# Experts' stage: router scores by token half, expert list before gates, residual and g2 moved into the PSUM sums

## The chip, the cores and the metric

The kernel runs on one core of one Trainium2 chip. The metric is the device time of one execution in microseconds (us), as the median of several executions; a profiled execution of its own gives the trace. Engine names in rows: PE is TensorE (PEld its weight loads), DVE is VectorE, ACT is ScalarE, POOL is GpSimd, SP is SyncE, whose queue (SPq) issues the weight loads.

## The reference, cut to what matters

The program runs two transformer blocks on 256 tokens of width 1024. The change touches only the last part, the mixture of experts of the second block and the final norm. `x` is the residual, `g2` one of six vectors of 1024 from the conditioning input, and everything is float32.

```python
h = rms_norm(x, norm2_w[l]) * (1.0 + sc2[:, None]) + sh2[:, None]
x = x + g2[:, None] * moe(h, w_router[l], router_bias[l], w_gate[l], w_up[l], w_down[l],
                          ws_gate[l], ws_up[l], ws_down[l])
return rms_norm(x, final_norm_w)
...
scores = jax.nn.sigmoid(xt.astype(jnp.float32) @ w_router.astype(jnp.float32))
sel = scores + router_bias.astype(jnp.float32)
group_score = lax.top_k(sel.reshape(M, N_GROUPS, N_EXPERTS // N_GROUPS), 2)[0].sum(-1)
_, gidx = lax.top_k(group_score, TOPK_GROUPS)
...
_, eidx = lax.top_k(jnp.where(emask, sel, -jnp.inf), TOP_K)
wts = jnp.take_along_axis(scores, eidx, axis=-1)
wts = wts / jnp.sum(wts, axis=-1, keepdims=True) * ROUTE_SCALE
...
routed = ...   # per token: sum over its 8 of 64 experts of gate * (silu(x w_gate) * (x w_up)) w_down
shared = (jax.nn.silu(xt @ ws_gate) * (xt @ ws_up)) @ ws_down
return (routed.reshape(M, D) + shared).reshape(B, T, D)
```

## The kernel before

Tokens lie in two halves of 128 (index `tt`). The function `moe` (line 1479 on) writes the instructions of PE, DVE, ACT and SP in program order: each of these engines runs its own list in the order in which the code issues it, and an instruction that waits holds up everything behind it on that engine.

The stage around the change runs in this order:

1. The normed tokens `h` are transposed into `hT` (`turn_in`), token half 0 first. The shared expert's first product (`shared_up(tt, b)`, line 1565; `b` counts four blocks of weights `wg`) starts for half 0 while half 1 is still normed.
2. The router scores (line 1617, PSUM tile `prt`) are one product of all 256 tokens with 64 experts. DVE copies them (`lg`, line 1623), PE turns them back to token rows (`prtT`), and ACT takes the sigmoid (`sc`, line 1628). Beside that ACT copies `h` into `hs[0]` and POOL computes the rest `hs[1]` (lines 1619 and 1620), which the gathers need later.
3. DVE picks groups and experts in some 30 small instructions: from `sel` (line 1651) to the mask `mk` (line 1684), then the gates (lines 1686 to 1691).
4. PE counts how many tokens each expert has (`ppos`, lines 1698 to 1702, from `mb`). DVE ranks the experts (`perm`), PE writes the list `plist` (lines 1774 and 1775), and DVE turns it into addresses `lst` (line 1779). SP reads `lst` (line 1825) before it can issue a load of an expert that is not one of the first three. A few small DVE instructions up to `moreu` (line 1788) say whether a rarely taken overflow branch is needed.
5. The shared expert is finished in between: `swiglu` (ACT at line 1576, DVE at line 1577), `turn` (two PE transposes `phT`, line 1583) and `shared_down`, which opens the four PSUM sums `psh` (named `py` in the rows).
6. `tables` and `gather` build the first unit's tokens (`pv`, line 1742; `pga`, line 1757), and `run` goes through the units: 25 units of up to 128 rows, of one to four experts each. A unit has four blocks of up products (`gu_unit`, line 1572), the down products two blocks (line 1591), and `combine` (line 1854), which adds it into the four PSUM sums. Its loads go through a ring of SBUF buffers in a fixed order: SP's next load waits until PE is done with the buffer it goes to.
7. At the end DVE and POOL multiply the four sums by `g2` (`mod[5]`) and add them to `x` (lines 1927 and 1929), and `final` norms `x` and writes it out.

Of the kernel before, what the change touches and what calls it, by code (L numbers as in the profile page):

```python
# [19 lines left out]
P = 128  # L20
# [1458 lines left out]
def moe(e, a, x, m, late, out):  # L1479
# [123 lines left out]
    for b in range(3):  # L1603
        shared_up(0, b)
# [9 lines left out]
    wr = wr.rearrange("p (c n) -> p c n", c=NC8)  # L1614
    p = ps.tile([P, 512], F32, tag="mm", name="prt", bufs=e.mm_bufs)
    for c in range(NC8):
        nc.tensor.matmul(p[:, :T], wr[:, c], hT[:, c], start=c == 0, stop=c == NC8 - 1)
    for tt in range(2):
        nc.scalar.activation(hs[0][:, tt], h[tt], AF.Copy)
        nc.gpsimd.tensor_sub(hs[1][:, tt], h[tt], hs[0][:, tt].bitcast(F32))  # L1620
    shared_up(0, 3)
# [8 lines left out]
    for b in range(4):  # L1630
        shared_up(1, b)
# [35 lines left out]
    hsh.append(turn(swiglu(pg[0])))  # L1667
    shared_down(0, 0)
# [16 lines left out]
    gate = pool.tile([P, 2, NE], F32, name="gate")  # L1685
    nc.vector.tensor_mul(gate, sc, mk)
    gsum = pool.tile([P, 2], F32, name="gsum")
    nc.vector.tensor_reduce(gsum, gate, axis=AX.X, op=OP.add)
    nc.vector.reciprocal(gsum, gsum)
    nc.vector.tensor_tensor(gate, gate, gsum[:, :, None].to_broadcast([P, 2, NE]), op=OP.mult)  # L1690
    nc.vector.tensor_scalar(gate, gate, 2.5, None, op0=OP.mult)

# [12 lines left out]
    shared_down(0, 1)  # L1705
# [70 lines left out]
    hsh.append(turn(swiglu(pg[1])))  # L1776
# [11 lines left out]
    nc.vector.tensor_copy(moreu, more)  # L1788
    for tt in range(2):
# [28 lines left out]
    def run(units, acc=(), new=None, ready=()):  # L1818
# [52 lines left out]
        for u in range(len(units) + 1):  # L1871
# [37 lines left out]
            if done is not None:  # L1909
# [12 lines left out]
        v = pool.tile([P, NC8, T], F32, tag="ehT", name=uid(e, "v"))  # L1922
        for tt in range(2):
            half = [slice(n * 512, (n + 1) * 512) for n in range(2)]
            vs = [v[:, 4 * tt + 2 * n:4 * tt + 2 * n + 2].rearrange("p a b -> p (a b)") for n in range(2)]
# [5 lines left out]
    def final():  # L1931
        for tt in range(2):
# [7 lines left out]
            for s in half:  # L1940
                nc.vector.scalar_tensor_tensor(o[:, s], x[tt][:, s], r, fw[:, s], op0=OP.mult, op1=OP.mult)
                nc.sync.dma_start(out[tt * P:(tt + 1) * P, s], o[:, s])

    run(units, psh, first_group, pre)
    final()
# [4 lines left out]
    if e.overflow:  # L1950
        with tc.If(nc.values_load(moreu[:, 5:6], min_val=0, max_val=T) > 0):
# [5 lines left out]
            with tc.If(v[2] > 0):  # L1957
                run([shared((r, 64), (r + 1, 64), base=64) for r in range(MID, LIGHT, 2)] 
# [6 lines left out]
            final()  # L1965
# [94 lines left out]
```

## Time and profile before

| what | value |
|---|---|
| median of 3 runs (lowest, highest) | 1731.15 us (1728.81, 1735.82) |
| the profiled execution's own time | 1730.54 us |
| its span in the trace | 1728.7 us |
| PE busy / PE weight loads busy | 1643.9 us (95%) / 1292.7 us (75%) |
| DVE busy / ACT busy / POOL busy | 1117.3 us (65%) / 745.1 us (43%) / 162.2 us (9%) |

The span is the profiled execution's time from its first to its last instruction; the own time is 1.8 us above it. The stage of the change, from the transposed tokens of half 0 to the first up product of an expert, takes from 1289.0 to 1325.8 us; the units run from there to about 1714 us, and the end takes the last 15 us.

### The profile page before, as it was taken

The numbers are of one execution on the slowest core, as the hardware profiler recorded it, in microseconds if no ns is written. First come the engines' busy times: TensorE is split into PE (matmuls) and PEld (weight loads), VectorE is DVE, ScalarE is ACT, GpSimd is POOL, SyncE is SP. The second block draws the span as 40 slices with busy tenths as digits, with TensorE's granted clock in tenths as the row PEclk, the third lists the DMA queues.
The fourth block names the chain that finished last, engine by engine and source line by source line (L and its number), as shares of the span: only waits on it lengthen the run. The fifth ranks groups of instructions, "written<-read, shape, count | busy, mean of one in ns | idle before, by whom it ended". The sixth has DMA issues, their size and how long they took to land.

```text
span 1728.7 us, 29531 instructions
## 1 busy us (share of the span) xinstructions
PE 1643.9 (95%) x11301; PEld 1292.7 (75%) x11301; DVE 1117.3 (65%) x2212; ACT 745.1 (43%) x1217; POOL 162.2 (9%) x84
## 2 busy tenths in 40 slices
PE   7999898999999999999899998998999999999996
PEld 7888798899989999787788876987875544444442
DVE  6765789994989999877777767689653111111113
ACT  4576444444544444444454455655542222222212
POOL 0000001232112122000000003024001000000000
PEclk9999999999999999999999999999999999999998
DMA  7442744456545555587888855442067799999994
GB/s 263 145 135 62 221 157 157 155 169 191 151 131 161 170 171 172 176 287 269 300 285 286 289 162 163 146 147 76 23 266 273 273 408 409 408 409 408 409 406 159
DMA packets 108118, 390.91 MB, mean 226 GB/s; under 512 B 12656, under 2 KB 12944, under 8 KB 107840
## 3 DMA queue, kind: packets, MB, share of 16 engines
q1 hardware_dynamic: 106128, 384.58, 63.7%
q0 software_dynamic: 976, 2.82, 0.6%
q8 instruction: 91, 1.49, 0.4%
q10 hardware_dynamic: 864, 1.53, 0.3%
q14 instruction: 59, 0.48, 0.1%
HBM read 386.79 MB, written 2.10 MB: 225 GB/s over the span
## 4 chain that ended last, share of the span: by engine, by line
PE 67%; DVE 17%; DMA 9%; issue 4%; ACT 3%; POOL 0%; DVEq 0%; SPq 0%; ACTq 0%
PE pgu L1572 10%; PE acc L696 8%; DMA raw<-in_w_ada 7%; PE py L1591 5%; PE pu L80 5%; PE pu L81 5%; PE pu L82 5%; DVE wlo L67 4%; PE pga L1757 3%; PE py L1854 3%; PE pg L642 2%; PE pmv L82 1%; PE pmv L80 1%; ACT whi L66 1%; PE pmv L81 1%
## 5 line engine op out<-in xcount | busy, mean ns | idle before, releaser
L66 ACT ACTIVATE whi<-raw 128x1024 fp32r<-128x1024 f32 x361 | 379.5, 1054 | 299.0 <-PE pu L81 138.5
L67 DVE TENSOR_TENSOR wlo<-raw,whi 128x1024 fp32r<-128x1024 f32 x315 | 385.2, 1226 | 81.3 <-ACT whi L66 80.3
L82 PE MATMUL pu<-pxT,wlo 128*128 128x256 f32 x1024 | 288.7, 282 | 11.6 <-DVE wlo L67 8.8
L80 PE MATMUL pu<-pxT,whi 128*128 128x256 f32 x1024 | 290.9, 284 | 0.7 <-ACT whi L66 0.7
L81 PE MATMUL pu<-pxT,whi 128*128 128x256 f32 x1024 | 287.5, 281 | 0.0
L696 PE MATMUL acc<-whi,hh 128*128 128x512 f32 x1008 | 279.6, 395 | 6.4 <-ACT hh L66 4.2
L696 PEld LDWEIGHTS acc<-whi,hh 128*128 128x128 f32 x1008 | 189.0, 189 | 51.3 <-DVE hh L67 5.2
L82 PEld LDWEIGHTS pu<-pxT,wlo 128*128 128x128 f32 x1024 | 194.0, 189 | 14.1 <-DVE wlo L67 10.9
L80 PEld LDWEIGHTS pu<-pxT,whi 128*128 128x128 f32 x1024 | 194.0, 189 | 0.9 <-ACT whi L66 0.9
L81 PEld LDWEIGHTS pu<-pxT,whi 128*128 128x128 f32 x1024 | 194.0, 189 | 0.0
L1572 PE MATMUL pgu<-raw,xg 128*32 128x512 f32 (+2 forms) x988 | 183.4, 597 | 0.0
L67 POOL TENSOR_TENSOR wlo<-raw,whi 128x1024 fp32r<-128x1024 f32 x46 | 128.1, 2788 | 499.6 <-ACT whi L66 498.1
L696 PE MATMUL acc<-wlo,hh 128*128 128x512 f32 x504 | 157.6, 393 | 2.2 <-DVE wlo L67 2.2
L66 ACT ACTIVATE hh<-H 128x256 fp32r<-128x256 f32 x126 | 52.6, 418 | 173.4 <-PE acc L696 171.6
L1572 PEld LDWEIGHTS pgu<-raw,xg 128*32 128x32 f32 (+2 forms) x988 | 52.4, 124 | 86.5 <-issue 74.9
L696 PEld LDWEIGHTS acc<-wlo,hh 128*128 128x128 f32 x504 | 94.8, 189 | 23.7 <-DVE wlo L67 3.8
L67 DVE TENSOR_TENSOR yl<-py,yh 128x512 fp32r<-128x512 f32 x50 | 34.6, 692 | 107.1 <-ACT yh L66 107.1
L1591 PE MATMUL py<-raw,th 128*32 128x512 f32 (+2 forms) x508 | 93.7, 596 | 0.5 <-ACT th L1585 0.5
L781 DVE SCALAR_TENSOR_TENSOR ada<-raw,cs,ada 128x1024 f32<-128x1024 f32 x48 | 61.5, 1282 | 41.0 <-DMA raw<-in_w_ada 40.9
L1577 DVE SCALAR_TENSOR_TENSOR hh<-hh,sv,pgu 128x256 f32<-128x256 f32 x25 | 12.0, 479 | 117.1 <-ACT hh L1576 117.1
L1760 ACT ACTIVATE xg<-pga 128x256 f32<-128x256 f32 (+1 forms) x104 | 39.1, 376 | 110.7 <-PE pga L1757 106.6
L1757 PEld LDWEIGHTS pga<-S,hs 128*128 128x128 f32 x416 | 54.8, 189 | 36.7 <-issue 36.0
(560 smaller groups left out, 2853.7 us busy)
## 6 DMA issues: line engine op xcount, KB each, us to landing
raw<-in_w_gu SPq DMA_DIRECT2D x187, 512.0 KB, 10.1
raw<-in_peer_u SPq DMA_DIRECT2D x128, 512.0 KB, 3.6
raw<-in_peer_v SPq DMA_DIRECT2D x128, 512.0 KB, 4.5
raw<-in_w_dn SPq DMA_DIRECT2D x91, 512.0 KB, 10.1
raw<-in_w_ada SPq DMA_DIRECT2D x48, 512.0 KB, 4.7
raw<-in_w_in_a SPq DMA_DIRECT2D x24, 512.0 KB, 3.9
raw<-in_w2a SPq DMA_DIRECT2D x17, 512.0 KB, 4.2
raw<-in_w_out SPq DMA_DIRECT2D x16, 512.0 KB, 3.5
```

The costliest lines, as they stand in the source:

```text
L66: e.nc.scalar.activation(hi, src, AF.Copy)
L67: (eng or e.nc.vector).tensor_sub(lo, src, hi.bitcast(F32))
L80: nc.tensor.matmul(out, lh, rh, start=first, stop=False)
L81: nc.tensor.matmul(out, lh, rl, start=False, stop=False)
L82: nc.tensor.matmul(out, ll, rh, start=False, stop=last)
L696: nc.tensor.matmul(acc[tt][n], h[l][:, s], w[r][:, n * 512:(n + 1) * 512], start=j == order[0] and i == 0, stop=j == order[-1] and i == 2)
L781: nc.vector.scalar_tensor_tensor(mod[n], w, cs[:, c:c + 1], mod[n], op0=OP.mult, op1=OP.add)
L1572: nc.tensor.matmul(pg[t], xx[:, c, t], ws[i][:, k * 512:(k + 1) * 512], start=c == 0, stop=c == NC8 - 1)
L1591: nc.tensor.matmul(py[q][t], th[:, k, t], w[i][:, q * 512:(q + 1) * 512], start=k == 0, stop=last and k == 1)
L1757: nc.tensor.matmul(p[:, :n].rearrange("p u n -> p (u n)"), hs[i][:, tt, q * P:(q + 1) * P], S[:, tt, :n].rearrange("p u n -> p (u n)"), st ...
L1760: nc.scalar.activation(xg[:, q, :n], p[:, :n], AF.Copy)
L1854: nc.tensor.matmul(acc[tt][n], St[:, tt * P:(tt + 1) * P], y[:, n * 512:(n + 1) * 512], start=first and v == 0 and w == 0, stop=v == len(u ...
```

## The change

The code changes in five places. The scores are computed by token half: half 0 ahead of the shared expert's first products, half 1 right after its transposes. The copies to `hs` go behind the sigmoid and an activation-table change. The shared products that stood ahead of the scores' way back are spread behind it. The gates, the shared down weights' multiplication by `g2` (new, in place, two 128x1024 instructions) and the first `swiglu` go behind the expert list. The residual `x` enters the PSUM sums by a product with the identity, each unit's result is multiplied by `g2` before it is split and added, and `final` reads the sums in PSUM.

```diff
-    for b in range(3):
+    def scores(tt):
+        for c in range(NC8):
+            nc.tensor.matmul(p[:, tts[tt]], wr[:, c], hT[:, c, tts[tt]], start=c == 0, stop=c == NC8 - 1)
+    scores(0)
+    for b in range(2):
         shared_up(0, b)
...
-    for c in range(NC8):
-        nc.tensor.matmul(p[:, :T], wr[:, c], hT[:, c], start=c == 0, stop=c == NC8 - 1)
-    for tt in range(2):
-        nc.scalar.activation(hs[0][:, tt], h[tt], AF.Copy)
-        nc.gpsimd.tensor_sub(hs[1][:, tt], h[tt], hs[0][:, tt].bitcast(F32))
-    shared_up(0, 3)
+    scores(1)
...
     warm(e, AF.Silu, sc[:, 0, 0:1])
-    for b in range(4):
-        shared_up(1, b)
+    for tt in range(2):
+        nc.scalar.activation(hs[0][:, tt], h[tt], AF.Copy)
+        nc.gpsimd.tensor_sub(hs[1][:, tt], h[tt], hs[0][:, tt].bitcast(F32))
+    for tt, b in ((0, 2), (0, 3), (1, 0)):
+        shared_up(tt, b)
...
     def shared_down(tt, k):
         if k == 0:
...
-        dn_block(psh[tt], hsh[tt], k, [(slice(0, P), 0)], [wd[k]], last=False)
+            for n in range(2):
+                nc.tensor.matmul(psh[tt][n], e.ident, x[tt][:, n * 512:(n + 1) * 512], start=True, stop=False)
+        for n in range(2):
+            nc.tensor.matmul(psh[tt][n], hsh[tt][:, k], wd[k][:, n * 512:(n + 1) * 512], start=False, stop=False)
...
-    hsh.append(turn(swiglu(pg[0])))
-    shared_down(0, 0)
...
-    gate = pool.tile([P, 2, NE], F32, name="gate")
-    nc.vector.tensor_mul(gate, sc, mk)
...
-    shared_down(0, 1)
+    shared_up(1, 1)
...
-    hsh.append(turn(swiglu(pg[1])))
...
+    gate = pool.tile([P, 2, NE], F32, name="gate")
+    nc.vector.tensor_mul(gate, sc, mk)
...
+    for k in range(2):
+        nc.vector.tensor_mul(wd[k], wd[k], mod[5])
+    hsh.append(turn(swiglu(pg[0])))
+    for b in (2, 3):
+        shared_up(1, b)
...
     first_group = tables(*select(units[:2]))
+    for k in range(2):
+        shared_down(0, k)
+    hsh.append(turn(swiglu(pg[1])))
...
-                    split(e, yh[:, sn], yl[:, sn], py[n])
+                    yg = wk.tile([P, 512], F32, tag="t5", name=uid(e, "yg"))
+                    nc.vector.tensor_mul(yg, py[n], mod[5][:, sn])
+                    split(e, yh[:, sn], yl[:, sn], yg)
...
-            for n, s in enumerate(half):
-                nc.vector.tensor_mul(vs[n], acc[tt][n], mod[5][:, s])
-            for n, eng in enumerate((nc.vector, nc.gpsimd)):
-                eng.tensor_add(x[tt][:, half[n]], x[tt][:, half[n]], vs[n])
...
-                nc.scalar.activation(o[:, s], x[tt][:, s], AF.Square, accum_out=ss[:, n:n + 1])
+                nc.scalar.activation(o[:, s], acc[tt][n], AF.Square, accum_out=ss[:, n:n + 1])
```

Behind `final`, two ACT and two DVE copies of the sums to `x` are new; they serve the overflow branch.

The first place is PE's list from the first shared product on. In the names, `prt` is the scores' tile, `pgu_14198` and `pgu_14199` are the shared expert's sums of token half 0 and 1, `ptr` the transposes of half 1, and `prtT` the scores' way back. Before:

```order
L1565 MATMUL pgu_14198<-raw_14034,ehT 128x512 x2
L1565 MATMUL pgu_14198<-raw_14036,ehT 128x512 x2
L1565 MATMUL pgu_14198<-raw_14115,ehT 128x512 x2
L1542 MATMUL ptr_14212<-ident,eh_14028 128x128 x4
L1542 MATMUL ptr_14218<-ident,eh_14028 128x128 x4
L1617 MATMUL prt<-ehT,raw_14117 128x256 x8
L1565 MATMUL pgu_14198<-raw_14210,ehT 128x512 x2
L1626 MATMUL prtT<-ident,lg 128x64 x2
```

Of the change:

```order
L1608 MATMUL prt<-ehT,raw_14117 128x128 x8
L1565 MATMUL pgu_14198<-raw_14034,ehT 128x512 x2
L1565 MATMUL pgu_14198<-raw_14036,ehT 128x512 x2
L1542 MATMUL ptr_14219<-ident,eh_14028 128x128 x4
L1542 MATMUL ptr_14225<-ident,eh_14028 128x128 x4
L1608 MATMUL prt<-ehT,raw_14117 128x128 x8
L1627 MATMUL prtT<-ident,lg 128x64 x2
L1565 MATMUL pgu_14198<-raw_14115,ehT 128x512 x2
```

Half of the scores moved ahead of the shared products, and `prtT` now follows the other half at once.

The second place is PE's list around the expert list (`plist`); `phT` are the transposes of the shared expert's activated product (of half 0 in the changed kernel, of half 1 in the one before), `py` the PSUM sums. Before:

```order
L1591 MATMUL py_14328<-raw_14258,th_14326 128x512
L1591 MATMUL py_14329<-raw_14258,th_14326 128x512
L1774 MATMUL plist<-perm,ecst 1x64
L1775 MATMUL plist<-perm,col 1x64
L1583 MATMUL phT_14383<-ident,hh_14380 128x128 x2
L1742 MATMUL pv_14410<-V_14366,S_14405 128x2 x4
```

Of the change:

```order
L1565 MATMUL pgu_14199<-raw_14036,ehT 128x512 x2
L1772 MATMUL plist<-perm,ecst 1x64
L1773 MATMUL plist<-perm,col 1x64
L1583 MATMUL phT_14388<-ident,hh_14385 128x128 x2
L1565 MATMUL pgu_14199<-raw_14115,ehT 128x512 x2
L1565 MATMUL pgu_14199<-raw_14217,ehT 128x512 x2
L1740 MATMUL pv_14406<-V_14349,S_14401 128x2 x4
L1655 MATMUL py_14415<-xb_12019,ident 128x512
L1655 MATMUL py_14416<-xb_12019,ident 128x512
L1657 MATMUL py_14415<-raw_14258,th_14391 128x512
```

The transposes of half 0, which stood ahead of `ppos`, now stand behind `plist`, with two shared products behind them, and the products with the identity are new behind `pv`.

The third place is DVE's list behind `moreu`; `raw_14258` and `raw_14260` are the shared down weights, `hh` is the activated product that `phT` turns. Of the change:

```order
L1785 CAST moreu<-more 1x6
L1787 TENSOR_TENSOR gate<-esc,mk 128x128
L1789 TENSOR_REDUCE gsum<-gate 128x2
L1790 RECIPROCAL gsum<-gsum 128x2
L1791 TENSOR_TENSOR gate<-gate,gsum 128x128
L1792 TENSOR_SCALAR gate<-gate 128x128
L1794 TENSOR_TENSOR raw_14258<-raw_14258,ada_9416 128x1024
L1794 TENSOR_TENSOR raw_14260<-raw_14260,ada_9416 128x1024
L1577 SCALAR_TENSOR_TENSOR hh_14385<-hh_14385,pgu_14198 128x256
L1799 COPY V_14349<-ecst 128x3
```

Before, the same stretch had no such instruction: `V` followed `moreu` at once.

```order
L1788 CAST moreu<-more 1x6
L1790 COPY V_14366<-ecst 128x3
L1791 COPY V_14366<-gate 128x3
L1790 COPY V_14366<-ecst 128x3
L1791 COPY V_14366<-gate 128x3
L1728 TENSOR_TENSOR S_14405<-io,num 128x2x128 x2
```

Eight instructions moved or new stand between `moreu` and `V`, and `hh_14385`, for which PE's `phT` waits, is the last of them.

## Rows read from the trace of the kernel before

**Rows 1.** Busy time by engine in two stretches of the units.
```profile
core 0: us, PE busy (x) PEld busy (x) DVE busy (x) ACT busy (x) POOL busy (x), PEclk, DMA share, GB/s
1340.00:1360.00 20.00, 20.00 (x98) 11.93 (x97) 3.03 (x7) 5.20 (x13) 0.00 (x0) 1.00 0.72 226
...
1660.00:1700.00 40.00, 40.00 (x222) 17.41 (x214) 5.11 (x8) 7.51 (x19) 0.00 (x0) 1.00 1.00 396
```

**Rows 2.** The chain of waits in the units: start, length, line, count.
```profile
1349.10 3.43 PE pgu L1572 x8
...
1363.38 3.57 PE pgu L1572 x32
```

**Rows 3.** Waits of PE's loads, and of SP's queue, in the units.
```profile
PEld pgu L1572 <- DMA raw<-in_w_gu: 4.3, 7, 0.8
...
SPq L1427 <- PE pgu L1572: 21.3, 27, 2.6
```

**Rows 4.** Timeline of PE in the stage: start, length, line, tiles, count.
```profile
1289.01 5.42 PE L1565 MATMUL pgu<-raw,ehT 128*128 128x512 f32 x12
...
1295.55 3.72 PE L1617 MATMUL prt<-ehT,raw 128*128 128x256 f32 x16 [0.25 <-ACT ehT L1543]
...
1301.19 7.13 PE L1565 MATMUL pgu<-raw,ehT 128*128 128x512 f32 x16
...
1310.84 0.22 PE L1698 MATMUL ppos<-mb,etri 128*128 128x64 bf16 x2
...
1315.53 1.02 PE L1742 MATMUL pv<-V,S 128*128 128x2 f32 x8 [1.64 <-DVE S L1728]
...
1325.83 3.60 PE L1572 MATMUL pgu<-raw,xg 128*128 128x512 f32 x8
```

**Rows 5.** Timeline of DVE, ACT and POOL in the stage.
```profile
1295.87 2.00 ACT L1619 ACTIVATE hs<-eh 128x1024 fp32r<-128x1024 f32 x2
1297.02 4.77 POOL L1620 TENSOR_TENSOR hs<-eh,hs 128x1024 fp32r<-128x1024 f32 x2 [2.24 <-ACT hs L1619]
...
1299.31 0.42 DVE L1623 COPY lg<-prt 64x256 f32<-64x256 f32 x1 [5.38 <-PE prt L1617]
...
1301.61 0.33 DVE L1651 TENSOR_TENSOR esel<-esc,rb 128x128 f32<-128x128 f32 x1 [1.88 <-ACT esc L1628]
...
1303.09 0.36 ACT L1576 ACTIVATE hh<-pgu 128x256 f32<-128x256 f32 x1
...
1305.02 0.17 DVE L1674 TENSOR_SCALAR gt<-gm 128x16 f32<-128x16 f32 x1
...
1306.85 0.29 DVE L1686 TENSOR_TENSOR gate<-esc,mk 128x128 f32<-128x128 f32 x1
...
1308.16 0.22 DVE L1695 CAST mb<-mk 128x128 bf16<-128x128 f32 x1
...
1313.56 0.34 DVE L1779 TENSOR_SCALAR lst<-plist 1x64 uint32<-1x64 f32 x2 [0.19 <-PE plist L1775]
...
1314.62 0.16 DVE L1788 CAST moreu<-more 1x6 uint32<-1x6 f32 x1
```

**Rows 6.** Timeline of an earlier stretch in which POOL and DVE overlap.
```profile
1141.15 2.40 POOL L67 TENSOR_TENSOR wlo<-raw,whi 128x1024 fp32r<-128x1024 f32 x1 [52.09 <-ACT whi L66]
...
1141.35 2.23 DVE L100 TENSOR_SCALAR rq<-ssq 128x8 f32<-128x8 f32 x1
```

**Rows 7.** Costliest groups of the page: count, busy, mean ns, idle before.
```profile
L67 DVE TENSOR_TENSOR wlo<-raw,whi 128x1024 fp32r<-128x1024 f32 x315 | 385.2, 1226 | 81.3 <-ACT whi L66 80.3
...
L67 DVE TENSOR_TENSOR yl<-py,yh 128x512 fp32r<-128x512 f32 x50 | 34.6, 692 | 107.1 <-ACT yh L66 107.1
```

**Rows 8.** Busy time around a gap of PE (columns as in Rows 1).
```profile
1182.00:1185.10 3.10, 0.01 (x2) 0.03 (x1) 3.10 (x6) 0.53 (x2) 0.89 (x1) 1.00 0.65 215
1185.10:1188.70 3.60, 3.60 (x12) 2.91 (x13) 3.20 (x9) 1.54 (x3) 0.00 (x0) 0.54 0.19 79
```

**Rows 9.** Timeline of the end.
```profile
1715.56 1.65 POOL L1929 TENSOR_TENSOR xb<-xb,v 128x512 f32<-128x512 f32 x1 [413.77 <-DVE v L1927]
...
1721.62 1.41 DVE L1941 SCALAR_TENSOR_TENSOR o<-xb,nr,ada 128x512 f32<-128x512 f32 x2
```

More of the change, by code (lines that the diff above doesn't have):

```diff
@@ L1601, in shared_up @@
         gu_block(pg[tt], hT[:, :, tts[tt]], b, wg[b])
-    for b in range(3):
+    wr = wr.rearrange("p (c n) -> p c n", c=NC8)
+    p = ps.tile([P, 512], F32, tag="mm", name="prt", bufs=e.mm_bufs)
+    def scores(tt):
[3 more added lines that the diff above has]
+    for b in range(2):
         shared_up(0, b)
@@ L1613, in moe @@
                                     ap=[[0, P], [1, D]]))
-    wr = wr.rearrange("p (c n) -> p c n", c=NC8)
-    p = ps.tile([P, 512], F32, tag="mm", name="prt", bufs=e.mm_bufs)
-    for c in range(NC8):
-        nc.tensor.matmul(p[:, :T], wr[:, c], hT[:, c], start=c == 0, stop=c == NC8 - 1)
-    for tt in range(2):
-        nc.scalar.activation(hs[0][:, tt], h[tt], AF.Copy)
-        nc.gpsimd.tensor_sub(hs[1][:, tt], h[tt], hs[0][:, tt].bitcast(F32))
-    shared_up(0, 3)
+    scores(1)
     lg = wk.tile([NE, T], F32, tag="lg", name="lg", bufs=1)
@@ L1684, in moe @@
     nc.vector.tensor_tensor(mk, mk, sel, op=OP.not_equal)
-    gate = pool.tile([P, 2, NE], F32, name="gate")
-    nc.vector.tensor_mul(gate, sc, mk)
[L1687 to L1691, printed above, removed]
     mb = pool.tile([P, 2, NE], BF, name="mb")
@@ L1788, in moe @@
     nc.vector.tensor_copy(moreu, more)
+    gate = pool.tile([P, 2, NE], F32, name="gate")
+    nc.vector.tensor_mul(gate, sc, mk)
+    gsum = pool.tile([P, 2], F32, name="gsum")
+    nc.vector.tensor_reduce(gsum, gate, axis=AX.X, op=OP.add)
+    nc.vector.reciprocal(gsum, gsum)
+    nc.vector.tensor_tensor(gate, gate, gsum[:, :, None].to_broadcast([P, 2, NE]), op=OP.mult)
+    nc.vector.tensor_scalar(gate, gate, 2.5, None, op0=OP.mult)
+    for k in range(2):
[3 more added lines that the diff above has]
+        shared_up(1, b)
     for tt in range(2):
@@ L1921, in run, with final @@
         combine(len(units) - 1, *y)
[L1922 to L1925, printed above, removed]
-            for n, s in enumerate(half):
-                nc.vector.tensor_mul(vs[n], acc[tt][n], mod[5][:, s])
-            for n, eng in enumerate((nc.vector, nc.gpsimd)):
-                eng.tensor_add(x[tt][:, half[n]], x[tt][:, half[n]], vs[n])
-    def final():
+        if first:
+            for tt in range(2):
+                for n in range(2):
+                    xs = x[tt][:, n * 512:(n + 1) * 512]
+                    nc.vector.tensor_add(xs, xs, acc[tt][n])
+        return acc
+    def final(acc):
         for tt in range(2):
@@ L1936, in final @@
             for n, s in enumerate(half):
-                nc.scalar.activation(o[:, s], x[tt][:, s], AF.Square, accum_out=ss[:, n:n + 1])
+                nc.scalar.activation(o[:, s], acc[tt][n], AF.Square, accum_out=ss[:, n:n + 1])
             nc.vector.tensor_add(ss[:, 0:1], ss[:, 0:1], ss[:, 1:2])
             r = rstd(e, wk, ss[:, 0:1], 1, 1.0 / D, "nr", True)
-            for s in half:
-                nc.vector.scalar_tensor_tensor(o[:, s], x[tt][:, s], r, fw[:, s], op0=OP.mult, op1=OP.mult)
+            for n, s in enumerate(half):
+                nc.vector.scalar_tensor_tensor(o[:, s], acc[tt][n], r, fw[:, s], op0=OP.mult, op1=OP.mult)
                 nc.sync.dma_start(out[tt * P:(tt + 1) * P, s], o[:, s])
-    run(units, psh, first_group, pre)
-    final()
+    acc = run(units, psh, first_group, pre)
+    final(acc)
+    if e.overflow:
+        for tt in range(2):
+            nc.scalar.activation(x[tt][:, :512], acc[tt][0], AF.Copy)
+            nc.vector.tensor_copy(x[tt][:, 512:], acc[tt][1])
     m.auto()
@@ L1964, in moe @@
                 run([shared((r, P), base=P) for r in range(WIDE)])
-            final()
+            final([[x[tt][:, n * 512:(n + 1) * 512] for n in range(2)] for tt in range(2)])
     ctx.close()
```

## Prediction

> **What bounds the kernel now.** I read the busy times of the units first, then the chain of waits, then the waits, and last the timeline of the stage that the change rewrites.
>
> In the units TensorE is busy all the time and the DMA engines nearly so: 20.00 of 20 us at a DMA share of 0.72 early on, 40.00 of 40 at 1.00 late [rows 1]. Busy time does not say which of the two sets the pace, so the reader is to look at the pitch. Thirty-two matmuls on 32 rows, four at a time side by side, take 3.57 us in the chain, and eight full ones 3.43 us [rows 2]. Both are eight steps of 0.43 us: a unit with four experts' weights runs at the pace of one with a single expert's. So TensorE is not stretched by loads. Its waits for up-product weights sum to 4.3 us over all units, while the load queue itself waited 21.3 us for TensorE to release buffers [rows 3]. In the early stretch the buffer ring is thus full and the loads follow TensorE. From this I conclude that the units start when the first up product starts (1325.83 [rows 4]) and move with it, one for one.
>
> In the stage ahead of them, 1289.0 to 1325.8, TensorE works most of the time: one 512-column matmul costs 7.13 / 16 = 0.44 us [rows 4]. The program writes two for each product, since float32 goes through in two passes (12 in the row for 6 in the order).
>
> **The change part by part.** I follow the time of the first `ppos` matmul, called T; it was 1310.84 [rows 4].
>
> *Scores in halves.* The 16 matmuls of 3.72 us become 2 x 16 on half the columns; I take half each, 1.86. Ahead of half 1's transposes stand 1.86 + 8 x 0.44 = 5.4 us, where 5.42 stood: no shift. The second half ends near 1295.55 + 1.86 = 1297.4 instead of 1299.3, and `lg` moves by -1.9 to 1297.4 [rows 4, 5]. Between `lg` and `esel` lay 2.30 us, of which some 1.0 was the way back waiting behind `shared_up(0, 3)` (1299.3 + 4 x 0.44 = 1301.0, against the copy's end at 1299.7). That goes: `esel` at about 1298.7, 2.9 earlier.
>
> *The selection chain.* From `esel` to the end of `mk` lay 5.24 us (1301.61 to 1306.85), of which about 0.4 was the `swiglu` that leaves. The gates' 1.31 (1306.85 to 1308.16) leave as well [rows 5]. Undisturbed, T would be 1298.7 + 4.8 + 0.3 (for `mb` and the hand-over) = 1303.8.
>
> *But the copies moved too.* GpSimd's two subtractions (4.77 us [rows 5]) ran while VectorE waited. Now ACT does sigmoid and table change first, is free 1.48 after `esel` (1303.09 - 1301.61), at 1300.2, and copies in 1.0 each. GpSimd starts 0.15 after the first copy, at about 1301.35, in the middle of the chain. What that does is seen earlier in the trace: a VectorE instruction on 128x8 elements, started 0.2 us after a GpSimd subtraction of this size, took 2.23 us and ended with it; undisturbed, the chain's 128x16 one takes 0.17 [rows 5, 6]. The same 128x16 instruction (`gt`, 3.4 after `esel`, less the 0.4 that leaves) would start at 1301.7 and wait for GpSimd until 1303.75. The second subtraction then holds it or a later one up to about 1306.2, and up to 1.8 us of the chain follow (1305.02 to 1306.85). The bounds are no wait and both subtractions, 4.8 us; I take 4.2 and T = 1308.0.
>
> *TensorE up to T.* After the way back it has 12 shared matmuls, 5.3 us, until 1303.6. It then idles 4.4 us until T.
>
> *From T to the list.* The list followed T by 2.72 us (1313.56), `moreu` ended 1.22 later [rows 5]. Now the gates follow (1.31), then two multiplications on 128x1024, priced by the float32 subtraction of that size at 1.23 each [rows 7], 2.45 in all, then the `swiglu`, 0.4. So `hh` is done at T + 8.1. TensorE's order has `phT` right behind the list, and two shared products that need none of this stand behind it. TensorE therefore idles from about T + 2.6 to T + 8.2, 5.6 us. Then come the transposes and 8 matmuls, 3.7, and `pv` starts at T + 11.9.
>
> *From `pv` to the units* lay 10.3 us (1315.53 to 1325.83 [rows 4]). Token half 0's sum now stands in it, 4 identity and 8 down matmuls, 5.3; half 1's transposes, 0.4; and 4 identity matmuls for half 1, 1.8: in all 17.8. The units start at T + 29.7, where it was T + 15.0.
>
> *The clock.* In an earlier gap TensorE did nothing for 3.1 us; in the 3.6 us behind it the granted clock was 0.54, near the lower of its two levels, 1.2 GHz [rows 8]. That loses 3.6 x 0.46 = 1.7 us. Both new gaps are longer. Behind the first the shared product ahead of the list doubles, about 1.3 us on the list; behind the second 1.7. The bounds are 0 and 3.4; I take 3.0, since the row's gap is the shorter.
>
> *Stage:* -2.8 (T) + 14.7 + 3.0 = +14.9 us, first up product near 1340.7.
>
> *In the units* two VectorE multiplications of 0.69 each [rows 7] join every unit; the result is used only after the next unit's up products, and VectorE is busy 5.11 of 40 us [rows 1]. I cost that at nothing; without that cover it would be 25 x 1.4 us.
>
> *The end.* The last unit has no cover: +1.4 for the multiplications, and ACT's table change, which stands behind the last split, moves with it. Multiplication (0.69), GpSimd's addition (1.65 [rows 9]) and the wait behind it go: -2.3 or more. I take -0.5. The bounds are -1.5 and +0.9: the new copies of the sums, two on VectorE, follow the last output instruction (start 1721.62 [rows 9]) and could delay the end.
>
> **Sum:** +14.4 on the profiled execution's 1730.5 is 1744.9. That execution is 0.6 below the median of the three runs, so I forecast 1745.
>
> **Rivals.**
>
> *The chain slips past GpSimd.* If VectorE gets ahead of the subtractions every time, T is 1303.8 and the first gap is 0.2: -7.0 + 14.7 + 1.7 - 0.5 = +8.9, 1740; without the slower clock 1738. For it: some instructions of the chain read one small tile only. Against it: an instruction of 128x8 was held the full time [rows 6]. The Trainium skill has this as a lock on a shared pair of ports (SBUF — State Buffer, Who interferes with whom): whichever of the two engines starts first keeps it for the whole instruction, so an order that favours VectorE would give this rival; the row shows the other order.
>
> *The stream of weights binds, and the earlier list is the gain.* Then the time goes with the list, 1313.56 before and T + 4.0 = 1312.0 now, or 1306.5 if VectorE slips past: -1.6 to -7.0, with the end 1723 to 1729. For it: a DMA share of 1.00 late [rows 1] and the remaining waits. Against it: the pitch and the queue's 21.3 us [rows 2, 3]. It decides only if the ring never fills before the units start to draw on it. The Trainium skill (Perfetto Trace Analysis, Identifying the Most-Contended Engine) warns that matmul busy time is a poor measure and asks for the weight loads' busy share. That is 17.41 of 40 us late [rows 1], which by this rule would point to the DMA engines and to this rival; the pitch speaks the other way, and I follow the pitch.
>
> *TensorE does not wait at `phT`*, because the moved work is cheaper than its rows say: half of the 5.6 us and its clock loss gone is -4.5, 1740.
>
> **How the numbers follow.** The forecast has 0.58, the first rival 0.18, the second 0.12, the third 0.08, and 0.04 goes to something faster that I do not see. A change of 0.5%, 8.7 us, is about what a measurement of this kernel can tell from none. The forecast is slower in every bound (1742 to 1748); the first and third rivals lie at the border and I split them evenly; the second counts as the same. Slower 0.58 + 0.13 = 0.71, the same 0.13 + 0.12 = 0.25, faster 0.04. The range 1736 to 1749 holds the forecast with its bounds and the first and third rivals, and leaves out the second.
>
> **What would show it.** In the changed trace: VectorE instructions of about 2 us while GpSimd subtracts; TensorE idle some 4 us before `ppos` and 5 to 6 before `phT`, a lower granted clock behind both; the first up product near 1340; the list near 1312 and the load queue waiting for TensorE soon after; the last output instruction about half a microsecond closer to the last down product. If the units start ten or more late and the time is unchanged, the conclusion from the pitch was wrong. If they start on time, a wait that I read from the order was not one.

## Result, and the profile after

The median of five runs of the changed kernel is 1747.83 us (1744.72 to 1752.68); five runs of the kernel before have 1735.46 (1728.81 to 1735.82). The medians lie 12.4 us apart. The ratio on record is 1.0093, 95% interval [1.0064, 1.0123]: slower by about 0.9%, by this ratio some 16 us. Forecast were 1745 us and 14 us.

The profiled execution after is the slowest of the five (1752.68, span 1750.9) and the one before lies below its median (1730.54, span 1728.7), so these two are further apart than the medians: 22.2 us by their spans. I therefore compare stretches inside an execution and not only its end. Four marks cut it: the first matmul of scores or shared products (start of the stage), the first up product of an expert, the start of the last down product, and the end of the span.

| us | before | after | difference | forecast |
|---|---|---|---|---|
| ahead of the stage (unchanged code) | 1289.01 | 1290.40 | +1.39 | 0 |
| stage, to the first up product | 36.82 | 51.97 | +15.15 | +14.9 |
| units, to the last down product | 383.21 | 387.60 | +4.39 | 0 |
| end | 19.66 | 20.93 | +1.27 | -0.5 |

The first row is no part of the change: in the eleven profiled executions of this study the stage starts anywhere from 1284.92 to 1295.60, behind the same code. This spread of about 10 us is of the size by which single runs of one kernel differ (13.3 us between the lowest and the highest of 17 runs of the kernel before).

In the stage, TensorE's timeline after answers to [rows 4]. The columns are start, duration, engine, line, instruction, count, and in brackets the idle time ahead and who ended it:

```profile
1309.59 0.22 PE L1696 MATMUL ppos<-mb,etri 128*128 128x64 bf16 x2 [4.34 <-DVE mb L1693]
...
1309.73 2.95 PE L1565 MATMUL pgu<-raw,ehT 128*128 128x512 f32 x4
1312.61 0.37 PE L1772 MATMUL plist<-perm,ecst 64*1 64x64 f32 x2
...
1318.41 0.69 PE L1583 MATMUL phT<-ident,hh 128*128 128x128 f32 x2 [5.21 <-DVE hh L1577]
1318.89 6.25 PE L1565 MATMUL pgu<-raw,ehT 128*128 128x512 f32 x8
1324.97 0.95 PE L1740 MATMUL pv<-V,S 128*128 128x2 f32 x8
1325.79 1.96 PE L1655 MATMUL py<-xb,ident 128*128 128x512 f32 x4
...
1342.37 3.17 PE L1572 MATMUL pgu<-raw,xg 128*128 128x512 f32 x7
```

Two gaps are new, 4.34 and 5.21 us, and behind each the wide matmuls are slow: four take 2.95 us where four ahead of the way back took 1.88 before, and eight take 6.25 where run three below has 3.60. How slow they are differs from one execution to the next: in runs six and eight, which have this code in the stage, the four take 3.76 and the eight 4.87 and 5.89, and the whole stage 51.52 and 52.61. The windows of the same stretch give the granted clock (the column behind POOL). It falls to 0.50, the lower level of 1.2 GHz, and is back at 1.00 only some 6 us behind the second gap:

```profile
1309.50:1312.60 3.10, 3.01 (x9) 0.97 (x9) 1.72 (x9) 0.00 (x0) 0.00 (x0) 0.67 0.00 0
1321.00:1323.00 2.00, 2.00 (x3) 0.67 (x2) 0.00 (x0) 0.00 (x0) 0.00 (x0) 0.50 0.94 356
1325.00:1328.00 3.00, 3.00 (x14) 1.82 (x13) 1.11 (x4) 0.38 (x1) 0.00 (x0) 1.00 0.97 382
```

VectorE and GpSimd in the stage, the rows that answer to [rows 5]:

```profile
1300.25 0.29 DVE L1659 TENSOR_TENSOR esel<-esc,rb 128x128 f32<-128x128 f32 x1 [0.73 <-ACT esc L1629]
...
1302.91 2.39 DVE L1676 TENSOR_TENSOR geq<-io,gf 128x64 f32<-128x64 f32 x1
1305.34 0.22 DVE L1678 TENSOR_REDUCE gm<-geq 128x16 f32<-128x64 f32 x1
1305.59 1.97 DVE L1680 TENSOR_SCALAR gt<-gm 128x16 f32<-128x16 f32 x1
...
1315.67 2.35 DVE L1794 TENSOR_TENSOR raw<-raw,ada 128x1024 f32<-128x1024 f32 x2
1317.94 0.41 DVE L1577 SCALAR_TENSOR_TENSOR hh<-hh,pgu 128x256 f32<-128x256 f32 x1
...
1302.85 4.67 POOL L1633 TENSOR_TENSOR hs<-eh,hs 128x1024 fp32r<-128x1024 f32 x2 [6.69 <-ACT hs L1632]
```

`esel` starts 9.85 us behind the stage's start where it was 12.60. Then `geq`, which starts 0.06 us behind the first subtraction on GpSimd, takes 2.39 us, and `gt` 1.97. Ahead of `phT` stand the gates, the two multiplications of the shared weights (2.35 together) and `hh`.

At the end, the timelines of VectorE, ACT and TensorE round the last-but-one unit's result and its combine:

```profile
1723.36 0.69 DVE L1930 TENSOR_TENSOR yg<-py,ada 128x512 f32<-128x512 f32 x1 [3.90 <-PE py L1591]
1724.80 0.69 DVE L67 TENSOR_TENSOR yl<-yg,yh 128x512 fp32r<-128x512 f32 x1 [0.76 <-ACT yh L66]
1725.41 0.68 DVE L1930 TENSOR_TENSOR yg<-py,ada 128x512 f32<-128x512 f32 x1
...
1724.14 0.63 ACT L66 ACTIVATE yh<-yg 128x512 fp32r<-128x512 f32 x1 [5.20 <-DVE yg L1930]
1726.13 0.63 ACT L66 ACTIVATE yh<-yg 128x512 fp32r<-128x512 f32 x1 [1.36 <-DVE yg L1930]
...
1720.48 3.64 PE L1591 MATMUL py<-raw,th 128*32 128x512 f32 x32
...
1724.82 0.49 PE L1866 MATMUL py<-yh,St 128*128 128x512 f32 x1 [0.28 <-ACT yh L66]
1726.81 0.66 PE L1866 MATMUL py<-yh,St 128*128 128x512 f32 x1 [1.50 <-ACT yh L66]
1728.13 1.06 PE L1866 MATMUL py<-yh,St 128*128 128x512 f32 x2
...
1729.97 3.85 PE L1591 MATMUL py<-raw,th 128*64 128x512 f32 x16
```

The second half's `yg` stands on VectorE behind the first half's `yl`, and that waits for ACT's `yh`. So the two copies start 1.99 us apart, and TensorE waits 1.50 inside the combine. The matmuls behind are slow again, 1.06 for two against 0.63 in the same place before. No up products stand between the last two results and their combines; in the units before them, they do. From the last-but-one unit's down product to the last one's (1720.48 to 1729.97) it takes 9.49 us; in the kernel before it was 6.49:

```profile
1702.55 3.64 PE L1591 MATMUL py<-raw,th 128*32 128x512 f32 x32
...
1708.01 0.63 PE L1854 MATMUL py<-yh,St 128*128 128x512 f32 x2
...
1709.04 3.65 PE L1591 MATMUL py<-raw,th 128*64 128x512 f32 x16
```

That is 3.00 of the 4.39 us by which the units grew. The other 1.39 arise at one place. The waits from the first up product on show what was waited for:

```profile
PEld pgu L1572 <- DMA raw<-in_w_gu: 5.1, 10, 0.8
PEld py L1591 <- DMA raw<-in_w_dn: 1.5, 2, 1.1
...
SPq L1427 <- PE pgu L1572: 23.5, 28, 3.3
```

The up products' weights are waited for about as long as in [rows 3] (4.3). The down products' weights are waited for 1.5 us instead of 0.5, all of it in the block that starts 316.1 us behind the first up product. Up to there every unit's down product stands within 0.13 us of its place before, counted from the first up product; the next one is 1.38 us late, and this stays. The load queue still waits for TensorE, 23.5 us (21.3 before): the units went with TensorE's start, as the prediction concluded from the pitch.

### The profile page after: what moved, and what is told of

The parts are those of the page before. It is cut to its first block, busy times and chain, and to the rows that moved or that the text cites. A ratio compares the mean times of both kernels' runs of the same rounds, so it can differ in the third digit from the quotient of the medians.

```text
span 1750.9 us, 29625 instructions
## 1 busy us (share of the span) xinstructions
PE 1656.9 (95%) x11325; PEld 1298.9 (74%) x11325; DVE 1151.9 (66%) x2260; ACT 747.5 (43%) x1219; POOL 157.8 (9%) x82
## 3 DMA queue, kind: packets, MB, share of 16 engines
q8 instruction: 91, 1.49, 0.4%
## 4 chain that ended last, share of the span: by engine, by line
PE 70%; DVE 17%; DMA 7%; ACT 3%; issue 3%; POOL 0%; DVEq 0%; SPq 0%; ACTq 0%
PE acc L696 11%; PE pgu L1572 10%; PE pu L80 5%; PE pu L82 5%; PE pu L81 5%; PE py L1591 5%; DMA raw<-in_w_ada 5%; DVE wlo L67 4%; PE pga L1755 3%; PE py L1866 3%; PE pg L642 2%; ACT whi L66 1%; PE pmv L80 1%; PE pmv L82 1%; PE pmv L81 1%
## 5 line engine op out<-in xcount | busy, mean ns | idle before, releaser
L80 PEld LDWEIGHTS pu<-pxT,whi 128*128 128x128 f32 x1024 | 196.6, 192 | 0.9 <-ACT whi L66 0.9
L81 PEld LDWEIGHTS pu<-pxT,whi 128*128 128x128 f32 x1024 | 196.8, 192 | 0.0
L66 ACT ACTIVATE yh<-yg 128x512 fp32r<-128x512 f32 x50 | 31.5, 630 | 164.2 <-DVE yg L1930 164.2
L1930 DVE TENSOR_TENSOR yg<-py,ada 128x512 f32<-128x512 f32 x50 | 34.4, 688 | 89.9 <-PE py L1591 89.9
L1591 PE MATMUL py<-raw,th 128*32 128x512 f32 (+2 forms) x492 | 87.3, 597 | 0.2 <-DMA raw<-in_w_dn 0.2
```

Of the source, the lines that this page charges most:

```text
L66: e.nc.scalar.activation(hi, src, AF.Copy)
L80: nc.tensor.matmul(out, lh, rh, start=first, stop=False)
L81: nc.tensor.matmul(out, lh, rl, start=False, stop=False)
L1591: nc.tensor.matmul(py[q][t], th[:, k, t], w[i][:, q * 512:(q + 1) * 512], start=k == 0, stop=last and k == 1)
```

## The experiments

Each is one look at one execution unless runs are given. I measure by the marks above, which the spread ahead of the stage doesn't touch.

**One: the turn behind the two shared products that need nothing.**

```diff
-    hsh.append(turn(swiglu(pg[0])))
     for b in (2, 3):
         shared_up(1, b)
+    hsh.append(turn(swiglu(pg[0])))
```

> The changed kernel with one move: the two transposes of the shared expert's first product (phT, with the swiglu ahead of them) stand behind the two shared products of half 1 instead of ahead of them; VectorE's order stays. If TensorE's second gap (5.2 us ahead of phT in the changed kernel, plus 2.6 us of slow matmuls behind it) is only a matter of what stands behind the waiting instruction, the stage from the first score to the first expert's up product falls from 52.0 us to about 46.5 (-5.5): 3.5 us of matmuls fill the gap, and the rest waits some 1.5 us. Rival: the wait just moves to pv, whose selection also comes late from VectorE; then the stage falls by 2 us at most, to 50 or more.

The stage took 48.76 us, 3.2 less than in the changed kernel; the wait is 1.54 instead of 5.21. That lies between the two expectations, and the timeline says why: the products that now fill the gap run at full speed, but what stands behind the rest of the wait does not, and the product ahead of the list took longer than in the profiled execution of the changed kernel (3.76 against 2.95).

```profile
1309.40 3.76 PE L1565 MATMUL pgu<-raw,ehT 128*128 128x512 f32 x4
...
1313.60 3.75 PE L1565 MATMUL pgu<-raw,ehT 128*128 128x512 f32 x8
1318.89 0.44 PE L1583 MATMUL phT<-ident,hh 128*128 128x128 f32 x2 [1.54 <-DVE hh L1577]
...
1320.41 3.64 PE L1655 MATMUL py<-xb,ident 128*128 128x512 f32 x4
```

Some 2.5 us of what the order gives back went to the clock at two other places: 0.8 in the product ahead of the list, 1.7 in the identity matmuls (3.64 for 1.96). Only the second can be due to the new order: the code up to the list is the changed kernel's, and runs six and eight have the same 3.76 there.

**Two: no subtractions on GpSimd.** This leaves out the low halves of the copies of h; they are set to zero instead.

```diff
+    nc.gpsimd.memset(hs[1].bitcast(F32), 0.0)
...
     for tt in range(2):
         nc.scalar.activation(hs[0][:, tt], h[tt], AF.Copy)
-        nc.gpsimd.tensor_sub(hs[1][:, tt], h[tt], hs[0][:, tt].bitcast(F32))
```

> The changed kernel without GpSimd's two subtractions: hs[1], the rest of the copy, is set to zero once, so the gathered tokens lose their low part. If GpSimd holds VectorE's selection chain, geq and gt fall from 2.39 and 1.97 us to about 0.2 each, ppos follows the 12 shared matmuls within 0.5 us instead of 4.3, the clock does not drop ahead of the list, and the stage falls from 52.0 us to about 46.6 (4.2 of wait and 1.1 of clock). Rival: the chain is slow by itself (its tiny instructions wait for one another); then these instructions and the stage stay within 0.5 us of the changed kernel's.

Stage 46.37 us, 5.6 less. The two held instructions are short, and TensorE waits 0.85 ahead of `ppos`. The wait at `phT` is the same 5.21, so the two gaps have separate causes. The zeros have a side effect: `esel` comes 0.47 us later against the stage's start than in the changed kernel, since it now waits for the router bias, whose load stands behind them on GpSimd.

```profile
1303.91 0.29 DVE L1659 TENSOR_TENSOR esel<-esc,rb 128x128 f32<-128x128 f32 x1 [1.21 <-DMA rb<-in_router_bias]
...
1306.57 0.23 DVE L1676 TENSOR_TENSOR geq<-io,gf 128x64 f32<-128x64 f32 x1
...
1307.08 0.17 DVE L1680 TENSOR_SCALAR gt<-gm 128x16 f32<-128x16 f32 x1
...
1309.29 0.22 PE L1696 MATMUL ppos<-mb,etri 128*128 128x64 bf16 x2 [0.85 <-DVE mb L1693]
...
1317.18 0.69 PE L1584 MATMUL phT<-ident,hh 128*128 128x128 f32 x2 [5.21 <-DVE hh L1578]
```

**Three: the gaps filled with matmuls that nobody reads.**

```diff
+    for _ in range(4):
+        nc.tensor.matmul(p, e.ident, x[0][:, :512], start=True, stop=True)
     wd = [load(a["ws_dn"][k], True) for k in range(2)]
...
     nc.tensor.matmul(pl[:, 1], col[:, 2:3], perm, start=True, stop=True)
+    for _ in range(5):
+        nc.tensor.matmul(p, e.ident, x[0][:, :512], start=True, stop=True)
```

> The changed kernel with matmuls that nobody reads put into TensorE's two gaps (4 products of 512 columns, 3.5 us, ahead of ppos; 5, 4.4 us, ahead of phT); VectorE's times stay. If the clock is what the gaps cost beyond themselves, the granted clock stays at 1.00, the product ahead of the list takes 1.8 us instead of 2.9 and the eight behind phT 3.6 instead of 6.1, and the stage falls from 52.0 us to about 48.3 (-3.7), although work was added. Rival: those matmuls are slow for another reason (they wait for data); then the stage stays at 52 or grows.

Stage 48.28 us, 3.7 less, though VectorE was held as long (2.41 and 2.03) and `ppos` came no earlier. The product ahead of the list takes 1.96 and the eight behind `phT` 3.60:

```profile
1307.73 1.96 PE L1565 MATMUL pgu<-raw,ehT 128*128 128x512 f32 x4
...
1315.76 3.60 PE L1565 MATMUL pgu<-raw,ehT 128*128 128x512 f32 x8
```

So the clock alone cost 3.7 us in the stage of the changed kernel's profiled execution; against the stages of runs six and eight it would be 3.2 and 4.3.

**Four: the new router order with the old end** (x and g2 outside the sums again; the diff undoes those hunks).

```diff
-                    yg = wk.tile([P, 512], F32, tag="t5", name=uid(e, "yg"))
-                    nc.vector.tensor_mul(yg, py[n], mod[5][:, sn])
-                    split(e, yh[:, sn], yl[:, sn], yg)
+                    split(e, yh[:, sn], yl[:, sn], py[n])
```

> The changed kernel's new order of the router stage with the old end: no identity products, no multiplication of the shared down weights or of the units' results by g2, x and g2 applied behind the last sum as before. Expected: the stage falls by the 8 identity matmuls (3.5) and the two VectorE multiplications ahead of phT (2.35) to about 46.1 us; from the first up product to the last down product 387.6 falls back by the 3.0 us in which the last-but-one sum waits for its result, to about 384.6 or less; from there to the end 20.9 falls to 19.7. Rival: the units are longer because the weights are late relative to TensorE after the late stage; then they stay at 387 with the old end.

Stage 45.85, units 383.29, end 19.64, and 1735.56 us in all. The units and the end are those of the kernel before: the first half of the change, with its late start, does not lengthen them by itself.

**Five: the other half alone.** The order of before in the router, with x and g2 in the sums.

```diff
+    wd = [load(a["ws_dn"][k], True) for k in range(2)]
+    for k in range(2):
+        nc.vector.tensor_mul(wd[k], wd[k], mod[5])
...
+                    yg = wk.tile([P, 512], F32, tag="t5", name=uid(e, "yg"))
+                    nc.vector.tensor_mul(yg, py[n], mod[5][:, sn])
+                    split(e, yh[:, sn], yl[:, sn], yg)
```

> The kernel before with the other half of the change alone: x as an identity product at the head of each token half's sum, the shared weights multiplied by g2, each unit's result multiplied by g2 before its splits, and the final step out of the sums. The router stands in the order of before; the two multiplications of the shared weights stand on VectorE ahead of lg, where it waits for the scores. Theory: this half costs in three places. Stage: eight more identity matmuls of 512 columns, 8 x 0.44 = 3.5 us, so 36.8 becomes about 40.3. Units: the last two combines wait for VectorE and ACT, and the loads start earlier against the units than in the changed kernel, so about 386.3 from the first up product to the last down product, against 383.2. End: about 20.3, against 19.7. In all about 7 us longer than the kernel before. Rival: the units' 4.4 us in the changed kernel came from the late start of the stage and the loads that ran into it, not from the multiplications; then the units here take 383 to 384.

Units 386.35 and end 20.33, as the theory had it, so the rival fell: of the 3.14 us over the kernel before, 3.00 lie between the last two down products, as in the changed kernel. In all 1741.19. The stage took 42.80, 2.5 more than expected. TensorE waits 1.64 us for `S` ahead of `pv`, exactly as in the kernel before [rows 4]; there `pv` behind it took 1.02, here it took 1.84, and what stands behind it runs at the lower level too:

```profile
1317.41 1.84 PE L1747 MATMUL pv<-V,S 128*128 128x2 f32 x8 [1.64 <-DVE S L1733]
...
1319.94 3.62 PE L1652 MATMUL py<-xb,ident 128*128 128x512 f32 x4
```

**Six: the last two results without g2.** The multiplication by g2 is left out for the last two units.

```diff
-                    yg = wk.tile([P, 512], F32, tag="t5", name=uid(e, "yg"))
-                    nc.vector.tensor_mul(yg, py[n], mod[5][:, sn])
+                    yg = py[n]
+                    if u < len(units) - 1:
+                        yg = wk.tile([P, 512], F32, tag="t5", name=uid(e, "yg"))
+                        nc.vector.tensor_mul(yg, py[n], mod[5][:, sn])
```

> The changed kernel, but the results of the last two units go to the splits without the multiplication by g2 (that part of the computation is left out). Theory: in every unit but these two the multiplications are hidden behind the next unit's up products. With them gone from the last two, the units from the first up product to the last down product shorten by about 1.5 (one wait of TensorE for a result of the last-but-one unit), and the end by about 1.5 (the last unit's), so units about 386 and end about 19.4; what is left of the units over 383.2 is waiting for weights. Rival: the two multiplications slow down every unit a little, by holding ACT or VectorE; then both stay as in the changed kernel, 387.6 and 20.9.

Units 384.32 and end 17.56: each is some 3.3 us shorter than in the changed kernel's profiled execution, twice what the theory said, and the rival fell. Of the 3.28 in the units, 3.00 lie between the last two down products, which stand 6.49 apart again, as in the kernel before. With 46 multiplications left in the units they take 1.1 more than before, all of it in the block 316 us behind the first up product, where the weights come late. And the new last step is worth 2.1 by itself (17.56 against 19.66) once no multiplication stands ahead of it.

**Seven: the order refitted.** The old end; scores in halves; no subtractions on GpSimd; every wait that the runs above had shown is given a product that needs nothing. The main edits, against the changed kernel:

```diff
+    for tt in range(2):
+        nc.scalar.activation(hs[0][:, tt], h[tt], AF.Copy)
+        nc.vector.tensor_sub(hs[1][:, tt], h[tt], hs[0][:, tt].bitcast(F32))
...
     scores(1)
+    shared_up(0, 2)
...
     nc.vector.tensor_copy(mb, mk)
+    hh = swiglu(pg[0])
...
-    shared_up(1, 1)
+    shared_up(1, 2)
+    hsh.append(turn(hh))
...
     nc.tensor.matmul(pl[:, 1], col[:, 2:3], perm, start=True, stop=True)
+    shared_up(1, 3)
+    for k in range(2):
+        shared_down(0, k)
```

> The new router order with the old end, and the waits that the experiments named filled: the scores' halves ahead, the copies and subtractions of h on ACT and VectorE in the wait for the scores (none on GpSimd), one shared product of half 0 between the second half of the scores and their way back, the swiglu of half 0 right behind mb, its transposes behind one shared product of half 1 ahead of the list, the last shared product and half 0's down products behind the list, the half 1 swiglu behind the first tables. Theory: the score halves themselves are worth their 2 to 3 us of an earlier selection when nothing waits behind them; from the first score to the first up product about 35.3 us against 36.8, units 383.2, end 19.7, in all 1 to 2 us faster than before, which lies within what the measurement tells from no change. Rival: in the stage TensorE's own work is the bound (about 34 us of it), so that an earlier list gains nothing: 36.8 or more, the time equal to before or a little longer.

The stage took 35.04 us, units 383.26, end 19.65 (1726.8 - 1707.15). The list comes 5.5 us earlier than before (18.68 behind the stage's start against 24.13), and of that 1.8 reaches the units, since TensorE works almost without a break:

```profile
1305.22 0.22 PE L1694 MATMUL ppos<-mb,etri 128*128 128x64 bf16 x2 [0.38 <-DVE mb L1690]
...
1305.37 1.96 PE L1565 MATMUL pgu<-raw,ehT 128*128 128x512 f32 x4
...
1307.53 0.27 PE L1771 MATMUL plist<-perm,ecst 64*1 64x64 f32 x2
```

Twelve runs have a median of 1733.29 us against 1735.86 of the kernel before (17 runs): ratio 0.9988 [0.9974, 1.0001]. That is no difference that the runs can tell, though the stage is 1.8 us shorter in the one trace.

**Eight: both multiplications of a unit ahead of its splits.**

```diff
                 for n in range(2):
-                    ...
-                    split(e, yh[:, sn], yl[:, sn], yg)
+                    nc.vector.tensor_mul(yg[n], py[n], mod[5][:, sn[n]])
+                for n in range(2):
+                    split(e, yh[:, sn[n]], yl[:, sn[n]], yg[n])
```

> The changed kernel, with one edit: both halves of a unit's result are multiplied by g2 before either half is split. In the changed kernel VectorE's second multiplication stands behind the first half's subtraction, which waits for ACT, so the second copy on ACT starts 1.99 us after the first. Theory: in the last two units this queue is most of what the multiplications cost; with both multiplications ahead, the second copy starts 0.65 after the first, 1.34 earlier. Units from the first up product to the last down product about 386.2 instead of 387.6, end 19.6 or less instead of 20.9 (down to 18.3 if TensorE's clock then holds). Rival: the cost is the multiplications themselves (2 x 0.69 a unit); then the order changes nothing, 387.6 and 20.9.

Units 384.36 and end 18.22: 3.2 and 2.7 us shorter than in the changed kernel's profiled execution, more than the 1.34 that the theory gave to the order. The second copy starts 0.80 behind the first, TensorE waits 0.30, and the granted clock in the stretch behind it is 1.00 where it was 0.50 (a window of the changed kernel's last-but-one combine, and then one of this kernel's):

```profile
1727.30:1730.00 2.70, 2.70 (x9) 1.54 (x7) 0.18 (x1) 0.00 (x0) 0.00 (x0) 0.50 0.02 6
```

```profile
1722.00:1725.50 3.50, 2.92 (x12) 1.43 (x12) 1.96 (x3) 1.44 (x3) 0.00 (x0) 1.00 0.02 5
```

The timeline of the same combine in this kernel:

```profile
1721.91 0.63 ACT L66 ACTIVATE yh<-yg 128x512 fp32r<-128x512 f32 x1 [5.20 <-DVE yg L1930]
1722.71 0.63 ACT L66 ACTIVATE yh<-yg 128x512 fp32r<-128x512 f32 x1 [0.17 <-DVE yg L1930]
...
1723.39 0.50 PE L1866 MATMUL py<-yh,St 128*128 128x512 f32 x1 [0.30 <-ACT yh L66]
```

Most of six's gain is here, with the multiplications in place. How much of it is the order and how much the clock, the earlier runs show. Runs one, two, three and five have the changed kernel's code in the units and at the end, and TensorE waits 1.48 or 1.49 us in the same place; in one and five the clock falls behind that wait, in two and three it holds there. Run two:

```profile
1724.03 0.50 PE L1866 MATMUL py<-yh,St 128*128 128x512 f32 x1 [1.49 <-ACT yh L66]
...
1725.10 0.63 PE L1866 MATMUL py<-yh,St 128*128 128x512 f32 x2
```

| kernel or run | last-but-one down product to the last, us |
|---|---|
| before, four, six, seven: no multiplication in the last two units | 6.48 to 6.49 |
| eight, nine: both multiplications first | 7.23 |
| two, three: half by half, the clock held | 8.41 to 8.42 |
| changed kernel, one, five: half by half, the clock fell | 9.49 |

So of the 3.00 us at this place the multiplications themselves cost 0.74, their order 1.19, and the clock 1.07. The rest of eight's gain in the units, 0.98, lies at the late weights, where this run is 0.40 behind the kernel before instead of 1.38. The end is 19.78 and 19.35 in runs two and three, 1.1 to 1.6 above run eight's.

**Nine: five with eight's order, and the identity matmuls of half 1 in the wait ahead of `pv`.**

```diff
     hsh.append(turn(swiglu(pg[1])))
+    head(1)
```

(`head` holds the identity matmuls that stood at the start of `shared_down`.)

> e5 with two edits: both multiplications of a unit ahead of its splits, and the identity matmuls of token half 1 moved to the place behind half 1's transposes, where TensorE waited 1.64 us for VectorE's S. Theory: the identity matmuls fill that wait, the clock does not fall behind it, and from pv to the first up product it takes the 10.3 us of the kernel before; stage about 27.7 + 10.3 = 38.0 instead of 42.8. Units about 385.0, end 18.3 to 19.0, in all about 1 to 2 us over the kernel before, which the measurement cannot tell from no change. Rival: the clock behind pv falls for another reason than the wait (in the kernel before TensorE waited the same 1.64 us there and kept its clock); then about 3 us of the slower stretch remain and the stage is about 41.

Stage 37.81, units 383.43, end 18.86. The wait is gone and with it the slow stretch:

```profile
1321.29 1.88 PE L1651 MATMUL py<-xb,ident 128*128 128x512 f32 x4
1323.09 1.02 PE L1749 MATMUL pv<-V,S 128*128 128x2 f32 x8
```

Ten runs have a median of 1733.94 against 1735.70 (13 runs), ratio 0.999 [0.9974, 1.0005]. This half of the change, well placed, costs nothing that can be told, and gives nothing either: +1.0 in the stage, +0.2 in the units, -0.8 at the end.

## Where the prediction held, and the step that failed

*The pitch.* The units went with the first up product, and the queue of loads kept waiting for TensorE (23.5 us). The rival by which the stream of weights binds has fallen: the list came earlier against the stage's start and the end came later. The Trainium skill (Perfetto Trace Analysis, Identifying the Most-Contended Engine) asks to judge TensorE by its weight loads' busy share and not by its matmul busy time. Read as in the prediction, that would have pointed to this rival; this trace does not bear the reading out, and the pitch of the matmuls was the better guide.

*Scores in halves.* `esel` came 2.75 us earlier, forecast 2.9.

*GpSimd ahead of VectorE.* Held were `geq` (2.39 - 0.23) and `gt` (1.97 - 0.17), 3.96 us in all; I took 4.2 between bounds of 0 and 4.8. The prediction named `gt` and what follows it; the first one held was `geq`, two instructions earlier, which GpSimd beat by 0.06 us. T moved by -2.64 (-2.8). Without the subtractions T came another 3.5 earlier (15.70 behind the stage's start against 19.19; the 0.47 by which `esel` came late there makes it 3.96) and the stage was 5.6 shorter, so this is shown. The rival by which the chain slips past did not occur, here or in runs one, three, four, six and eight, where `geq` and `gt` are held for the same time (2.39 to 2.43 and 1.96 to 2.03). The Trainium skill (SBUF — State Buffer, Who interferes with whom) says that the engine that issues first keeps the shared pair for a whole instruction, and that a reduction on VectorE doesn't contend. The trace agrees with both: `gm`, a reduction between the two held instructions, took 0.22 us while GpSimd was at work, as long as in run two without the subtractions.

*The two gaps and the wait at `phT`.* 4.34 and 5.21, forecast 4.4 and 5.6. From `pv` to the units it took 17.40, forecast 17.8. The rival by which TensorE does not wait at `phT` fell.

*The clock.* 3.7 by run three, taken 3.0 between 0 and 3.4. Mis-sized by 0.7, and above its own bound: the bound was made of one stretch of 3.6 us behind each gap, but behind the second the lower level lasted 6 us. The stage as a whole came out 0.25 from the forecast (+15.15 against +14.9). So close a hit is luck: the small errors cancel, and the same code gave +14.70 and +15.79 in runs six and eight.

*Where it failed.* The step is the one that says of the two multiplications in the units, "I cost that at nothing", with its companion "The last unit has no cover: +1.4". Measured are +4.39 in the units and +1.27 at the end, where 0 and -0.5 stood (the end's upper bound was +0.9): 6.2 us above the forecast in the profiled execution, and 3.3 to 5.2 in runs one, two, three and five, whose units and end have the same code. Two things were overlooked. First, not one unit lacks cover but two. The premise that "the result is used only after the next unit's up products" doesn't hold for the last-but-one unit: the last up products stand ahead of its down product, so TensorE has nothing to do between that result and its combine. Second, I counted the multiplications by their length (1.4) and not by their place in VectorE's queue, where the second one stands behind a subtraction that waits for ACT. The order sets the second copy 1.19 us back (1.99 behind the first against 0.80 in run eight), and in three of five executions the wait that it makes on TensorE is followed by matmuls at half speed. By run eight's table this step cost 3.00 us in the units: 0.74 for the multiplications, 1.19 for their order, 1.07 for the clock. At the end, run eight's 18.22 against 19.35 to 20.93 in the five executions puts 1.1 to 2.7 on order and clock together. The remaining 1.39 in the units is TensorE waiting for one block's weights. It is 0.8 to 1.4 in the changed kernel and in runs one, two, three and six, 0.4 in eight, at most 0.14 in four, five and seven, and -0.5 in nine. So neither the late stage alone (four) nor the multiplications alone (five) brings it; why those weights come late stays open.

*The whole.* By the profiled pair the change costs 20.8 us without the stretch ahead of the stage; by the ratio 16, by the medians 12.4. The difference between these I put down to the spread of single executions, but that was not settled: there is one profiled execution of each. So the total near the forecast of 14 is partly luck, since the marks show costs that the forecast did not hold.

## What to carry to other kernels

Moving work to an engine that seems idle is to be priced by the queue it joins: the second half's multiplication, issued behind the first half's subtraction, makes a chain through two engines, and issuing both multiplications first took 1.19 us out of it. Look for the units at the end of a loop that have no successor to cover them, and count them by the order of the program. A wait on TensorE is worth filling even where nothing comes earlier by it, since the matmuls behind it may run at half speed, and an earlier result gains only what the busiest engine's own work leaves: the list came 5.5 us earlier in run seven and 1.8 of it arrived.

## What the runs showed of the hardware

TensorE's clock does not follow from the length of a wait alone. Behind the same wait of 1.64 us, between the same instructions, `pv` took 1.02 us in the kernel before and 1.84 in run five; behind 1.54 us in run one the transposes and `pv` kept full speed and the identity matmuls after them lost it. At the end, behind the same wait of 1.49 us in the same code, the clock held in runs two and three and fell in the changed kernel and in runs one and five (1.48 there). What tells these cases apart stays open; filling the wait kept the clock in every run that tried it (three, seven and nine).

The stage's start varied over 10.7 us between executions of the same code ahead of it, more than half of what the change did. Marks inside an execution gave repeatable numbers where TensorE waited little (units of 383.21 to 383.43 us in four kernels), where the total of a single run would have misled. Where it waited, they varied too: the changed kernel's code took 386.16 to 387.60 us in the units and 19.35 to 20.93 at the end in five executions, so a difference of 1 us there needs more than one look.
